# Expert rows in a two-layer network: stores on GpSimd's queue, gathers two pairs ahead in buffers of their own, the short stream first

## The chip, the cores and the metric

The kernel runs on one core of one Trainium2 chip. The metric is the device time of one execution in microseconds (us). In the profile PE is TensorE (PEld its weight loads), DVE is VectorE, ACT is ScalarE, POOL is GpSimd and SP is SyncE, which here only issues DMAs. A queue such as SPq or ACTq is the part of an engine that issues them.

## What is computed

The network has two blocks. The change touches the end of each of the two layers of the second block: a feed-forward part in which 16 experts each choose the tokens that they like best.

```
def _expert_choice_ffn(h, w_router, w_gate, w_up, w_down):
    b, t, d = h.shape
    cap = EC_CAPACITY_FACTOR * t // N_EXPERTS
    aff = jax.nn.softmax(jnp.einsum('btd,de->bte', h, w_router).astype(jnp.float32), axis=-1)
    vals, idx = lax.top_k(aff.transpose(0, 2, 1), cap)
    xg = jax.vmap(lambda hb, ib: hb[ib])(h, idx)
    hid = jax.nn.silu(jnp.einsum('becd,edf->becf', xg, w_gate)) * jnp.einsum('becd,edf->becf', xg, w_up)
    out = jnp.einsum('becf,efd->becd', hid, w_down) * vals[..., None].astype(h.dtype)
    return jax.vmap(lambda ob, ib: jnp.zeros((t, d), h.dtype).at[ib.reshape(-1)].add(ob.reshape(-1, d)))(out, idx)
```

The main stream x has 512 tokens of width 1024, so an expert takes 64 of them. The short stream cx (the context) has 256 tokens and an expert takes 32. Layer 0 runs the experts for both streams with the same weights; layer 1 needs only x. The result is scaled by a gate and added to the stream.

## The kernel before

All arithmetic of the experts is float32. Their weights are read from HBM once for each layer: for each pair of experts 8 pieces of 1 MB for gate and up, and 4 for down, 96 pieces in a layer. `ffn` sets the order: `gate_up` of pair 0, then for each further pair q its `gate_up` and `down` of pair q-1, and at last `down` of pair 7. The pieces go through SP's queue into a ring of slots: EW buffers of their own, and three more that lie in the memory of x and cx themselves, which are free once the streams have been written to HBM. A piece can only be issued when the matmuls on the piece that had its slot are done.

Before the experts, `route` works out the choices. ACT writes every token's row twice into an HBM tensor: scaled by its norm (`normed`, L1564) and as it is (`acc`, L1565; in layer 1 that is the output itself). DVE finds the best tokens by rounds of MAX8, FIND_INDEX8 and MATCH_REPLACE8, and makes the lists `gi` (rows to gather) and `si` (rows to add to).

For a pair, `gathered` (L1653) fetches the 128 rows of its two experts from `normed` by an indirect DMA on GpSimd's queue; PE transposes them (L1659) and ACT modulates them (L1662). In layer 0 one more gather on every second pair fetches the rows of cx for four experts. `gate_up` runs the matmuls of x (L1707) and of cx (L1716), `hidden` the activation, `down` those of x (L1730) and cx (L1742). DVE scales them (L1733, L1748) and `scatter` (L1762) adds them to `acc` by two indirect DMAs for each stream, also on GpSimd's queue; a scatter waits until the one before it into the same tensor has landed. After layer 0, `reload` reads the sums back (L1774), squares them on ACT (L1776) and transposes them on PE (L1780), the short stream first, and one `rsqrt` for all six row tiles follows. Then the mixers of layer 1 begin with matmuls at L472.

A scheduler at build time decides the order of instructions on each engine. It also gives each DMA one of eight completion counters: eight for the DMAs that SP and ACT issue together, and eight others for those of GpSimd. A DMA waits until the one that last had its counter has landed, whoever issued that one.

All row buffers (two in `route`, a gather's, a scatter's, two in `reload`) come from one pool of six, `row`.

Of the kernel before, what the change touches and what calls it, by code (L numbers as in the profile page):

```python
# [16 lines left out]
OP = mybir.AluOpType  # L17
# [204 lines left out]

EW = 12
FILL_NA = (0, 1) * 6
FILL_H = (1, (0, 1, 0, 1, 0, 1, 0), 1, 0)

# [6 lines left out]
class _K:  # L235
# [1287 lines left out]
    def route(self, l, v, x, nt, cap, state, got):  # L1523
# [30 lines left out]
        wk = self.tl("y", [16, 512])[:, :W]  # L1554
        yield
        for i in range(nt):
            raw, row = self.tl("row", [P, D]), self.tl("row", [P, D])
            for s in range(2):
                pq = self.pt("s")
                for k in range(4):  # L1560
                    ten.transpose(pq[:, k * P:(k + 1) * P], x[:, 4 * s + k, i * P:(i + 1) * P], self.idf)
                act.activation(row[:, s * 512:(s + 1) * 512], pq, AF.Copy, scale=rs[:, i:i + 1])
                act.activation(raw[:, s * 512:(s + 1) * 512], pq, AF.Copy)
            act.dma_start(self.normed[v][i * P:(i + 1) * P, :], row)  # L1564
            act.dma_start(self.acc[v][i * P:(i + 1) * P, :], raw)  # L1565

        val = self.s1(f"val{v}", [16, cap])
        idx = self.s1(f"idx{v}", [16, cap], U32)
# [77 lines left out]
        if need:  # L1646
            self.reload(x, cx)

    def gathered(self, l, v, gi, n):

        nc = self.nc
        row = self.tl("row", [P, D])
        nc.gpsimd.indirect_dma_start(row[:], None, self.normed[v][:, :], bass.IndirectOffsetOnAxis(ap=gi[:, n:n + 1], axis=0))  # L1653
        o = self.tl("xg", [P, KT, P])
        a2, b2 = self.mods[v]
        for s in range(2):
            pq = self.pt("t")
            for k in range(4):
                nc.tensor.transpose(pq[:, k * P:(k + 1) * P], row[:, (4 * s + k) * P:(4 * s + k + 1) * P], self.idf)  # L1659
            for k in range(4):  # L1660
                d = 4 * s + k
                nc.scalar.activation(o[:, d], pq[:, k * P:(k + 1) * P], AF.Identity, scale=a2[:, d:d + 1], bias=b2[:, d:d + 1])  # L1662
        return o

    def experts(self, l, acts, got, eload):
# [3 lines left out]
        ten, vec, act, pool = nc.tensor, nc.vector, nc.scalar, nc.gpsimd  # L1669
        self.mods = {v: self.mod_cols(l, v, 3, self.v(f"n2{l}")) for v in got}  # L1670
        two = 1 in got
        xg, hid = {}, {}

        def inputs(q):
            if q < 8:
                xg[0, q] = self.gathered(l, 0, got[0][0], q)
                if two and q % 2 == 0:
                    xg[1, q] = xg[1, q + 1] = self.gathered(l, 1, got[1][0], q // 2)

        def hidden(q, v, g, u, n):  # L1680

# [15 lines left out]
        def gate_up(q):  # L1697
            pg, pu = self.pt("g"), self.pt("g")
            pv = self.pt("o") if two else None
            x0 = xg[0, q]  # L1700
            for j in range(2):
                w = [[eload() for _ in range(2)] for _ in range(2)]
                for ps, wn in ((pg, w[0]), (pu, w[1])):
                    for k in range(4):
                        d = 4 * j + k
                        for e in range(2):
                            ten.matmul(ps[e * 64:(e + 1) * 64], x0[:, d, e * 64:(e + 1) * 64], wn[e][:, k],  # L1707
                                       start=d == 0, stop=d == 7)
                if two:
                    for k in range(4):  # L1710
                        d = 4 * j + k
                        for n in range(2):
                            for e in range(2):
                                r = (2 * n + e) * 32
                                c = (2 * (q % 2) + e) * 32
                                ten.matmul(pv[r:r + 32], xg[1, q][:, d, c:c + 32], w[n][e][:, k],  # L1716
                                           start=d == 0, stop=d == 7)
            hidden(q, 0, pg, pu, P)
            if two:
                hidden(q, 1, pv[:64], pv[64:], 64)  # L1720

        def down(q):
            w = [[eload() for _ in range(2)] for _ in range(2)]
            gi, si, val, gate = got[0]
            y = self.tl("row", [P, D])
            for j in range(2):
                ps = self.pt("s")
                for f in range(4):
                    for e in range(2):
                        ten.matmul(ps[e * 64:(e + 1) * 64], hid[0, q][:, f, e * 64:(e + 1) * 64], w[j][e][:, f],  # L1730
                                   start=f == 0, stop=f == 3)
                c = slice(j * 512, (j + 1) * 512)
                vec.scalar_tensor_tensor(y[:, c], ps, val[:, q:q + 1], gate[:, c], OP.mult, OP.mult)  # L1733
            self.scatter(0, y, si, q, 64)
            if two:
                gi, si, val, gate = got[1]
                ps = self.pt("a")
                for f in range(4):
                    for j in range(2):
                        for e in range(2):  # L1740
                            r = (2 * j + e) * 32
                            ten.matmul(ps[r:r + 32], hid[1, q][:, f, e * 32:(e + 1) * 32], w[j][e][:, f],  # L1742
                                       start=f == 0, stop=f == 3)
                y = self.tl("row", [P, D])
                for j in range(2):
                    r = slice(j * 64, j * 64 + 64)
                    c = slice(j * 512, (j + 1) * 512)
                    vec.scalar_tensor_tensor(y[:64, c], ps[r], val[r, q:q + 1], gate[r, c], OP.mult, OP.mult)  # L1748
                self.scatter(1, y, si, q, 32)

        inputs(0)
        for what, q in acts:
            if what == "gu":
                inputs(q + 1)
                gate_up(q)
            else:
                down(q)
# [8 lines left out]
    def reload(self, x, cx):  # L1766

        nc = self.nc
        ss = self.s1("ssr", [P, 6])
        ev = 0  # L1770
        for v, xs, nt, c0 in ((1, cx, 2, 0), (0, x, 4, 2)):
            for i in range(nt):
                row = self.tl("row", [P, D])
                nc.scalar.dma_start(row, self.acc[v][i * P:(i + 1) * P, :])  # L1774
                j = self.tl("row", [P, D])
                nc.scalar.activation(j, row, AF.Square, accum_out=ss[:, c0 + i:c0 + i + 1])  # L1776
                for s in range(2):
# [2 lines left out]
                        nc.tensor.transpose(pq[:, k * P:(k + 1) * P], row[:, (4 * s + k) * P:(4 * s + k + 1) * P], self.idf)  # L1780
                    d = xs[:, 4 * s:4 * s + 4, i * P:(i + 1) * P]
                    nc.vector.tensor_copy(d, pq.rearrange("p (k c) -> p k c", k=4))
        self.rsqrt(ss, 6, 1.0 / D, self.rs2)

    def block2(self, x, cx, rb, dram, out):
        self.rs2 = self.one("rs2", [P, 6])
        for l in range(DEPTH):
            need = l < DEPTH - 1
            with self.scope(v=3, z2=4, n=1, e3=5, sb=1, f3=9, h=16, t=5, tg=2, xc=1, wr=2, wh=2, wl=2, sm=2, s1=1):
                states = self.mixer2(l, x, cx, need, *rb)  # L1790
            self.normed = [dram.tile([n, D], F32, name=f"normed{l}{n}", tag=f"n{n}") for n in ((T, 256) if need else (T,))]
            self.acc = [dram.tile([n, D], F32, name=f"acc{l}{n}", tag=f"a{n}") for n in (T, 256)] if need else [out]
            with self.scope(ew=EW, row=6, xg=4, hid0=2, **({"hid1": 2} if need else {}), t=5, sm=2, s1=1):
                self.ffn(l, x, cx, need, states)
            rb = None, self.rs2

# [46 lines left out]
```

## Time and profile before

| what | us |
|---|---|
| median of 3 runs (3087.5 to 3098.31) | 3091.7 |
| the profiled execution | 3086.54 |
| its span, first to last instruction | 3084.8 |
| PE busy | 2844.5 (92%) |
| DVE busy | 1493.4 (48%) |
| ACT busy | 1164.3 (38%) |
| POOL busy | 256.3 (8%) |

The span is what the trace shows; 1.74 us of the execution lie around it. All times below are us from the start of the span. The experts of layer 0 run from about 2001 to 2339, the reload up to 2383, the mixers of layer 1 to 2795, its route and experts to the end. Busy PE is an average over stages with different limits, so each stage has to be read by itself.

### The profile page before, as it was taken

The page shows a single profiled execution, that of the slowest core. Times are in us where ns is not written, and L with a number is a line of the kernel's source. Part 1 is how long each engine was busy: PE and PEld are TensorE (multiplying, and loading weights), DVE is VectorE, ACT ScalarE, POOL GpSimd, SP SyncE. Part 2 cuts the span into 40 slices and gives each one's busy share as a digit, 9 for nine tenths or more (in the row PEclk, how much of TensorE's full clock was granted, in tenths as well). Part 3 has the DMA queues.
Part 4 walks back from the last instruction along what each step waited for, and adds up shares of the span by engine and source line. Part 5 has one row for each costly group of instructions (what it writes and reads, how often), then busy time and mean ns, then how long its engine had stood idle before and what let it go on. Part 6 is the DMA issues. An engine that isn't in the chain of part 4 may idle for free. (4 is left out here: it accounts for less than half of the span.)

```text
span 3084.8 us, 46595 instructions
## 1 busy us (share of the span) xinstructions
PE 2844.5 (92%) x18975; PEld 1935.1 (63%) x18976; DVE 1493.4 (48%) x3039; ACT 1164.3 (38%) x2410; POOL 256.3 (8%) x236
## 2 busy tenths in 40 slices
PE   8999999999999999999999999798896999996985
PEld 5676667876776667877766888523223767773321
DVE  4625686544535686636366466611113465574100
ACT  5523454433533454444454342421112463443210
POOL 0000031000000020100011010011111010000111
PEclk9999999999999999999999999799997999997999
DMA  4142424412233224421110111778884111118998
GB/s 146 48 167 73 143 97 171 151 60 71 69 123 115 97 97 163 164 83 50 48 33 28 56 43 36 287 282 328 322 325 112 54 42 52 51 51 339 410 406 308
DMA packets 97574, 439.54 MB, mean 142 GB/s; under 512 B 11216, under 2 KB 12496, under 8 KB 72784
## 3 DMA queue, kind: packets, MB, share of 16 engines
q1 hardware_dynamic: 86976, 401.09, 35.2%
q0 software_dynamic: 6640, 21.83, 3.1%
q10 hardware_dynamic: 3744, 13.63, 1.2%
q8 instruction: 150, 2.46, 0.3%
q14 instruction: 64, 0.52, 0.1%
HBM read 416.40 MB, written 20.97 MB: 142 GB/s over the span
## 5 line engine op out<-in xcount | busy, mean ns | idle before, releaser
L472 PE MATMUL psg<-h,wh 128*128 128x512 f32 x1616 | 653.1, 405 | 2.4 <-ACT z L1322 1.9
L473 PE MATMUL psg<-h,wh 128*128 128x512 f32 x1616 | 647.4, 401 | 0.0
L474 PE MATMUL psg<-h,wl 128*128 128x512 f32 x1616 | 646.9, 400 | 0.0
L462 DVE TENSOR_TENSOR wl<-wr,wh 128x1024 fp32r<-128x1024 f32 (+2 forms) x272 | 338.7, 1246 | 489.0 <-ACT wh L460 477.5
L460 ACT ACTIVATE wh<-wr 128x1024 fp32r<-128x1024 f32 (+2 forms) x272 | 281.0, 1034 | 606.9 <-PE psg L473 528.0
L472 PEld LDWEIGHTS psg<-h,wh 128*128 128x128 f32 x1616 | 305.1, 189 | 95.8 <-issue 24.6
L473 PEld LDWEIGHTS psg<-h,wh 128*128 128x128 f32 x1616 | 305.0, 189 | 74.5 <-issue 14.3
L474 PEld LDWEIGHTS psg<-h,wl 128*128 128x128 f32 x1616 | 305.3, 189 | 73.6 <-issue 12.4
L1707 PE MATMUL psg<-ew,xg 128*64 128x512 f32 x832 | 235.0, 629 | 16.9 <-DMA ew<-in_eu_dram 11.4
L472 PE MATMUL psg<-y,wh 128*128 128x256 f32 (+1 forms) x560 | 181.0, 324 | 2.7 <-ACT y L448 2.0
L473 PE MATMUL psg<-y,wh 128*128 128x256 f32 (+1 forms) x560 | 180.3, 322 | 0.0
L474 PE MATMUL psg<-y,wl 128*128 128x256 f32 (+1 forms) x560 | 178.5, 319 | 0.0
L1707 PEld LDWEIGHTS psg<-ew,xg 128*64 128x64 f32 x832 | 68.4, 144 | 150.2 <-issue 118.7
L1684 DVE SCALAR_TENSOR_TENSOR t<-t,psg 128x512 f32<-128x512 f32 x16 | 11.0, 688 | 306.2 <-ACT t L1683 306.2
L1662 ACT ACTIVATE xg<-pst,mB,mA 128x128 f32<-128x128 f32 x160 | 58.6, 466 | 164.9 <-PE pst L1659 164.8
L1007 ACT ACTIVATE t<-pst 128x512 f32<-128x512 f32 (+1 forms) x134 | 69.9, 557 | 125.4 <-PE pst L1004 122.5
L472 PEld LDWEIGHTS psg<-y,wh 128*128 128x128 f32 x560 | 107.0, 191 | 16.2 <-ACT y L448 2.4
L472 PE MATMUL psg<-f,wh 128*128 128x256 f32 (+1 forms) x360 | 113.3, 316 | 4.0 <-DVE x L557 1.8
L1730 PE MATMUL pss<-ew,hid 128*64 128x512 f32 x416 | 108.8, 598 | 5.3 <-DMA ew<-in_ed_dram 5.3
L473 PE MATMUL psg<-f,wh 128*128 128x256 f32 (+1 forms) x360 | 112.7, 313 | 0.8 <-DVE f L1242 0.8
L473 PEld LDWEIGHTS psg<-y,wh 128*128 128x128 f32 x560 | 107.3, 192 | 9.5 <-issue 2.1
L474 PE MATMUL psg<-f,wl 128*128 128x256 f32 (+1 forms) x360 | 111.5, 310 | 0.0
(462 smaller groups left out, 4489.8 us busy)
## 6 DMA issues: line engine op xcount, KB each, us to landing
ew<-in_eg_dram SPq DMA_DIRECT2D x52, 1024.0 KB, 12.0
ew<-in_eu_dram SPq DMA_DIRECT2D x52, 1024.0 KB, 11.7
ew<-in_ed_dram SPq DMA_DIRECT2D x52, 1024.0 KB, 11.3
wm<-in_wm_dram SPq DMA_DIRECT2D x96, 512.0 KB, 4.4
wr<-in_w_f_dram SPq DMA_DIRECT2D x92, 512.0 KB, 3.6
wr<-in_v_f_dram SPq DMA_DIRECT2D x60, 512.0 KB, 3.2
wr<-in_w_o_dram SPq DMA_DIRECT2D x32, 512.0 KB, 3.8
x<-in_eg_dram SPq DMA_DIRECT2D x10, 1024.0 KB, 14.4
```

The costliest lines, as they stand in the source:

```text
L460: nc.scalar.activation(hi, raw, AF.Copy)
L462: nc.vector.tensor_tensor(lo, raw, hi, OP.subtract)
L472: t.matmul(ps, a[0], b[0], start=first, stop=False)
L473: t.matmul(ps, a[0], b[1], start=False, stop=False)
L474: t.matmul(ps, a[1], b[0], start=False, stop=last)
L1007: self.nc.scalar.activation(pT[:, :w], pp[:, :w], AF.Copy)
L1662: nc.scalar.activation(o[:, d], pq[:, k * P:(k + 1) * P], AF.Identity, scale=a2[:, d:d + 1], bias=b2[:, d:d + 1])
L1684: vec.scalar_tensor_tensor(th, th, 1.0, g, OP.add, OP.mult)
L1707: ten.matmul(ps[e * 64:(e + 1) * 64], x0[:, d, e * 64:(e + 1) * 64], wn[e][:, k], start=d == 0, stop=d == 7)
L1730: ten.matmul(ps[e * 64:(e + 1) * 64], hid[0, q][:, f, e * 64:(e + 1) * 64], w[j][e][:, f], start=f == 0, stop=f == 3)
```

## The change

Six things change. (1) The stores of rows to `normed` and `acc` are issued by GpSimd instead of ACT. (2) Row buffers are two pools of four: `in` for raw rows, gathers and reloads, `row` for scaled rows and scatters. EW goes from 12 to 11, which makes room. (3) The gathers of pair q+2 are issued at the start of pair q, apart from their transposes. (4) In `gate_up` and `down` the short stream's matmuls stand ahead of the main stream's. (5) So its scatter does too. (6) `reload` has a `rsqrt` for each stream.

```
-EW = 12
+EW = 11
...
-            raw, row = self.tl("row", [P, D]), self.tl("row", [P, D])
+            raw, row = self.tl("in", [P, D]), self.tl("row", [P, D])
...
-            act.dma_start(self.normed[v][i * P:(i + 1) * P, :], row)
-            act.dma_start(self.acc[v][i * P:(i + 1) * P, :], raw)
+            nc.gpsimd.dma_start(self.normed[v][i * P:(i + 1) * P, :], row)
+            nc.gpsimd.dma_start(self.acc[v][i * P:(i + 1) * P, :], raw)
...
+    def gather(self, v, gi, n):
+
+        row = self.tl("in", [P, D])
+        self.nc.gpsimd.indirect_dma_start(row[:], None, self.normed[v][:, :],
+                                          bass.IndirectOffsetOnAxis(ap=gi[:, n:n + 1], axis=0))
+        return row
...
+        def fetch(q):
+            for v in range(1 + (two and q % 2 == 0)):
+                if q < 8:
+                    rows[v, q] = self.gather(v, got[v][0], q // 2 if v else q)
+
         def inputs(q):
...
+            for v in range(1 + (two and q % 2 == 0)):
+                if q < 8:
+                    xg[v, q] = xg[v, q + v] = self.modulated(v, rows.pop((v, q)))
...
+        fetch(0)
+        fetch(1)
         inputs(0)
         for what, q in acts:
             if what == "gu":
+                fetch(q + 2)
                 inputs(q + 1)
                 gate_up(q)
...
-                row = self.tl("row", [P, D])
+                row = self.tl("in", [P, D])
...
-        self.rsqrt(ss, 6, 1.0 / D, self.rs2)
+            c = slice(c0, c0 + nt)
+            self.rsqrt(ss[:, c], nt, 1.0 / D, self.rs2[:, c])
...
-            with self.scope(ew=EW, row=6, xg=4, hid0=2, **({"hid1": 2} if need else {}), t=5, sm=2, s1=1):
+            with self.scope(ew=EW, row=4, **{"in": 4}, xg=4, hid0=2, **({"hid1": 2} if need else {}), t=5, sm=2, s1=1):
```

Three places in the order of instructions matter below. The first is SP's queue at the beginning of layer 0's experts. `ew`, `x` and `cx` are the slots of weight pieces, `wr` a weight of the mixer ahead. DMAHW0 to 7 are the counters shared by SP and ACT, DMASW0 to 7 those of GpSimd; the number behind them has no meaning here. Before:

```order
L458 DMA wr_18119<-in_v_o_dram 128x768 [waits DMAHW1_49,DVE_49]
L1626 DMA ew_18234<-in_eg_dram 128x2048
L1626 DMA ew_18236<-in_eg_dram 128x2048 [waits DMAHW5_49,PE_49]
L1626 DMA ew_18238<-in_eu_dram 128x2048 [waits DMAHW6_49,DMASW1_49,Pool_49]
L1626 DMA ew_18240<-in_eu_dram 128x2048
L1626 DMA ew_18242<-in_eg_dram 128x2048 [waits DMAHW2_49]
L1626 DMA ew_18244<-in_eg_dram 128x2048 [waits DMAHW5_49,Pool_49]
L1626 DMA ew_18246<-in_eu_dram 128x2048 [waits DMAHW6_49]
L1626 DMA ew_18248<-in_eu_dram 128x2048 [waits DMAHW1_49]
L1626 DMA ew_18250<-in_eg_dram 128x2048 [waits DMAHW3_49]
L1626 DMA ew_18252<-in_eg_dram 128x2048 [waits DMAHW5_49]
```

And in the changed kernel:

```order
L458 DMA wr_17987<-in_v_o_dram 128x768 [waits DMAHW7_49,DVE_49]
L1626 DMA ew_18237<-in_eg_dram 128x2048
L1626 DMA ew_18239<-in_eg_dram 128x2048 [waits DMASW1_49,DVE_49,Pool_49]
L458 DMA wr_18049<-in_v_o_dram 128x768 [waits DMAHW0_49,DVE_49]
L1626 DMA ew_18241<-in_eu_dram 128x2048 [waits DMAHW5_49,PE_49]
L458 DMA wr_18119<-in_v_o_dram 128x768 [waits DMAHW6_49,DMAHW1_49,DVE_49]
L1626 DMA ew_18243<-in_eu_dram 128x2048
L1626 DMA ew_18245<-in_eg_dram 128x2048 [waits Pool_49]
L1626 DMA ew_18247<-in_eg_dram 128x2048
L1626 DMA ew_18249<-in_eu_dram 128x2048 [waits DMAHW2_49]
L1626 DMA ew_18251<-in_eu_dram 128x2048 [waits DMAHW3_49]
L1626 DMA ew_18253<-in_eg_dram 128x2048 [waits DMAHW4_49]
```

In the changed kernel the weight pieces take the counters one after the other (2, 3, 4), and the first three stand ahead of the last two loads of the mixer; before, they skip counters, which ACT's stores hold.

The second place is GpSimd's queue in the first pairs of layer 0. Names with 18206 and 18208 belong to the main stream, with 18207 and 18209 to the short one. Before:

```order
L1762 DMA acc_18208<-row_18866,si_3791_18510 512x1024
L1653 DMA row_18911<-normed_18206,gi_3790_18508 128x1024
L1762 DMA acc_18208<-row_18866,si_3791_18510 512x1024
L1762 DMA acc_18209<-row_18906,si_3796_18528 256x1024 x2
L1762 DMA acc_18208<-row_19044,si_3791_18510 512x1024
L1653 DMA row_19089<-normed_18206,gi_3790_18508 128x1024
L1762 DMA acc_18208<-row_19044,si_3791_18510 512x1024
L1762 DMA acc_18209<-row_19084,si_3796_18528 256x1024
L1653 DMA row_19110<-normed_18207,gi_3795_18526 128x1024
L1762 DMA acc_18209<-row_19084,si_3796_18528 256x1024
```

And in the changed kernel:

```order
L1564 DMA normed_18207<-row_18471 128x1024
L1565 DMA acc_18209<-in_18470 128x1024
L1652 DMA in_18567<-normed_18206,gi_3789_18509 128x1024
L1652 DMA in_18569<-normed_18207,gi_3794_18527 128x1024
L1652 DMA in_18571<-normed_18206,gi_3789_18509 128x1024
L1652 DMA in_18611<-normed_18206,gi_3789_18509 128x1024
L1652 DMA in_18613<-normed_18207,gi_3794_18527 128x1024
L1652 DMA in_18725<-normed_18206,gi_3789_18509 128x1024
L1652 DMA in_18916<-normed_18206,gi_3789_18509 128x1024
L1652 DMA in_18918<-normed_18207,gi_3794_18527 128x1024
L1652 DMA in_19096<-normed_18206,gi_3789_18509 128x1024
L1774 DMA acc_18209<-row_18888,si_3795_18529 256x1024 x2
```

The gathers (now L1652) up to pair 5 stand ahead of the first scatter (now L1774), and behind the last of twelve stores; before, the gather for the next pair stood behind a scatter of this one.

The third place is ACT's queue in `reload`. Before:

```order
L1774 DMA row_20057<-acc_18209 128x1024
L1776 ACTIVATE row_20059,ssr_20056<-row_20057 128x1024
L1774 DMA row_20073<-acc_18209 128x1024
L1776 ACTIVATE row_20075,ssr_20056<-row_20073 128x1024
L1774 DMA row_20089<-acc_18208 128x1024
L1776 ACTIVATE row_20091,ssr_20056<-row_20089 128x1024
```

And in the changed kernel:

```order
L1785 DMA in_20059<-acc_18209 128x1024
L1785 DMA in_20075<-acc_18209 128x1024
L1785 DMA in_20111<-acc_18208 128x1024
L1787 ACTIVATE row_20061,ssr_20058<-in_20059 128x1024
L1787 ACTIVATE row_20077,ssr_20058<-in_20075 128x1024
L1787 ACTIVATE row_20113,ssr_20058<-in_20111 128x1024
L1785 DMA in_20127<-acc_18208 128x1024
L1785 DMA in_20143<-acc_18208 128x1024
L1785 DMA in_20159<-acc_18208 128x1024
L1787 ACTIVATE row_20129,ssr_20058<-in_20127 128x1024
```

The loads go out three at a time; before, each waited behind the square of the row before it.

## Rows read from the trace of the kernel before

**Rows 1.** What PE waited for, 1955 to 2345: total us, times, longest.

```profile
PE pst L1659 <- DMA row<-normed,gi: 30.3, 8, 5.5
```

**Rows 2.** Chain that ended last, 2150 to 2345: start, us, what.

```profile
...
2212.46 10.61 DMA row<-normed,gi
...
2280.91 2.72 PE pss L1730 x10
...
2314.65 2.72 PE pss L1730 x10
...
```

**Rows 3.** PE in order of time, start of layer 0's experts.

```profile
...
2012.67 1.09 PE L1659 MATMUL pst<-const_sb,row 128*128 128x128 f32 x4 [5.49 <-DMA row<-normed,gi]
...
2020.33 3.65 PE L1707 MATMUL psg<-ew,xg 128*64 128x512 f32 x14
...
2041.77 1.20 PE L1659 MATMUL pst<-const_sb,row 128*128 128x128 f32 x8
...
2064.41 2.79 PE L1730 MATMUL pss<-ew,hid 128*64 128x512 f32 x10
...
```

**Rows 4.** What SP's queue waited for, whole span.

```profile
...
SPq L1626 <- DMA acc<-row: 44.5, 4, 26.2
...
SPq L1626 <- DMA out_dram<-row: 25.9, 3, 19.9
...
```

**Rows 5.** SP's queue in order of time.

```profile
...
1912.45 23.04 SPq L458 DMA_DIRECT2D wr<-in_v_o_dram  x5
...
1945.67 26.90 SPq L1626 DMA_DIRECT2D ew<-in_eu_dram  x2
...
2840.49 0.33 SPq L1626 DMA_DIRECT2D ew<-in_eu_dram  x1
...
```

**Rows 6.** Stretches: length, busy PE, PEld, DVE, ACT, POOL, clock, DMA share, GB/s.

```profile
1945.00:1970.00 25.00, 21.93 (x152) 16.74 (x150) 17.35 (x58) 10.33 (x21) 0.00 (x0) 1.00 0.44 181
1970.00:2001.00 31.00, 12.96 (x78) 9.31 (x78) 23.13 (x73) 12.85 (x24) 1.03 (x1) 0.55 1.00 382
...
2028.00:2281.00 253.00, 230.18 (x1278) 75.75 (x1276) 32.80 (x46) 43.33 (x105) 34.46 (x27) 0.95 0.88 329
...
2841.00:3058.00 217.00, 184.72 (x802) 61.97 (x798) 20.76 (x29) 26.99 (x64) 21.13 (x16) 0.98 1.01 406
```

**Rows 7.** POOL in order of time.

```profile
1991.21 1.03 POOL L1653 DMA_INDIRECT row<-normed,gi  x1 [100.92 <-DVE y L1575]
2008.27 0.97 POOL L1653 DMA_INDIRECT row<-normed,gi  x1 [16.03 <-DMA cx<-in_eu_dram]
...
2341.64 1.41 POOL L1762 DMA_INDIRECT acc<-row,si  x1 [3.55 <-DMA acc<-row,si]
...
2344.24 1.10 POOL L1137 DMA_DIRECT2D f<-in_namask_dram  x1
...
2824.14 1.03 POOL L1653 DMA_INDIRECT row<-normed,gi  x1 [81.64 <-DMA normed<-row]
```

**Rows 8.** PE in order of time, end of layer 0's experts and reload.

```profile
...
2335.55 3.62 PE L1742 MATMUL psa<-ew,hid 128*32 128x512 f32 x26
...
2383.19 0.80 PE L472 MATMUL psg<-y,wh 128*128 128x256 f32 x2 [2.03 <-ACT y L448]
...
```

**Rows 9.** ACT and its queue in order of time, around layer 0's experts.

```profile
...
1946.09 0.85 ACT L460 ACTIVATE wh<-wr 128x768 fp32r<-128x768 f32 x1
...
1968.26 0.34 ACTq L1564 DMA_DIRECT2D normed<-row  x1
...
2353.23 0.33 ACTq L1774 DMA_DIRECT2D row<-acc  x1
...
2374.51 1.06 ACT L1776 ACTIVATE row<-row 128x1024 f32<-128x1024 f32 x1 [3.06 <-DMA row<-acc]
...
```

**Rows 10.** DVE in order of time, last list of layer 0's route, list of layer 1's.

```profile
...
1996.05 0.16 DVE L1592 CAST gi<-pst 128x4 uint32<-128x4 f32 x1 [0.75 <-PE pst L1588]
...
2820.62 0.17 DVE L1592 CAST gi<-pst 128x8 uint32<-128x8 f32 x1 [0.94 <-PE pst L1588]
...
```

More of the change, by code (lines that the diff above doesn't have):

```diff
@@ L1647, in ffn, with modulated @@
             self.reload(x, cx)
-    def gathered(self, l, v, gi, n):
+    def gather(self, v, gi, n):
[3 more added lines that the diff above has]
+        return row
+    def modulated(self, v, row):
         nc = self.nc
-        row = self.tl("row", [P, D])
-        nc.gpsimd.indirect_dma_start(row[:], None, self.normed[v][:, :], bass.IndirectOffsetOnAxis(ap=gi[:, n:n + 1], axis=0))
         o = self.tl("xg", [P, KT, P])
@@ L1671, in experts @@
         two = 1 in got
-        xg, hid = {}, {}
+        rows, xg, hid = {}, {}, {}
+        def fetch(q):
+            for v in range(1 + (two and q % 2 == 0)):
+                if q < 8:
+                    rows[v, q] = self.gather(v, got[v][0], q // 2 if v else q)
         def inputs(q):
[L1675 to L1678, printed above, removed]
+            for v in range(1 + (two and q % 2 == 0)):
+                if q < 8:
+                    xg[v, q] = xg[v, q + v] = self.modulated(v, rows.pop((v, q)))
         def hidden(q, v, g, u, n):
@@ L1702, in gate_up @@
                 w = [[eload() for _ in range(2)] for _ in range(2)]
[L1703 to L1708, printed above, removed]
                 if two:
@@ L1717, in gate_up @@
                                            start=d == 0, stop=d == 7)
+                    if j:
+                        hidden(q, 1, pv[:64], pv[64:], 64)
+                for ps, wn in ((pg, w[0]), (pu, w[1])):
+                    for k in range(4):
+                        d = 4 * j + k
+                        for e in range(2):
+                            ten.matmul(ps[e * 64:(e + 1) * 64], x0[:, d, e * 64:(e + 1) * 64], wn[e][:, k],
+                                       start=d == 0, stop=d == 7)
             hidden(q, 0, pg, pu, P)
-            if two:
-                hidden(q, 1, pv[:64], pv[64:], 64)
         def down(q):
             w = [[eload() for _ in range(2)] for _ in range(2)]
[L1724 to L1734, printed above, removed]
             if two:
@@ L1749, in down @@
                 self.scatter(1, y, si, q, 32)
+            gi, si, val, gate = got[0]
+            y = self.tl("row", [P, D])
+            for j in range(2):
+                ps = self.pt("s")
+                for f in range(4):
+                    for e in range(2):
+                        ten.matmul(ps[e * 64:(e + 1) * 64], hid[0, q][:, f, e * 64:(e + 1) * 64], w[j][e][:, f],
+                                   start=f == 0, stop=f == 3)
+                c = slice(j * 512, (j + 1) * 512)
+                vec.scalar_tensor_tensor(y[:, c], ps, val[:, q:q + 1], gate[:, c], OP.mult, OP.mult)
+            self.scatter(0, y, si, q, 64)
+        fetch(0)
+        fetch(1)
         inputs(0)
@@ L1769, in reload @@
         ss = self.s1("ssr", [P, 6])
-        ev = 0
         for v, xs, nt, c0 in ((1, cx, 2, 0), (0, x, 4, 2)):
             for i in range(nt):
-                row = self.tl("row", [P, D])
+                row = self.tl("in", [P, D])
                 nc.scalar.dma_start(row, self.acc[v][i * P:(i + 1) * P, :])
```

## Prediction

> **What bounds the kernel now.** I read the waits of PE first, since PE is busy for 92% of the span and what it waits for is where time can come from. Around layer 0's experts it waits mainly for one thing, the gathered rows: 30.3 us in eight pieces, none over 5.5 [rows 1]. The chain of waits says why a gather is late. It stands on GpSimd's queue behind a scatter, and under the weight traffic it takes up to 10.61 us to land; the next transposes wait for it [rows 2]. The same chain has what a pair costs without a gather: between the `down` of pairs 5 and 6 lies only the `gate_up` of pair 7, for which nothing more is gathered, and that is 2314.65 - 2280.91 = 33.74 us [rows 2]. PE in order of time gives a pair with gathers: the first `down` begins at 2064.41 [rows 3], five pairs before 2280.91, so (2280.91 - 2064.41) / 5 = 43.3 us.
>
> Next I read SP's waits, because SP carries all weights. It waited 44.5 us in layer 0 and 25.9 us in layer 1 for stores that ACT had issued [rows 4]. No weight piece reads what these stores write; what the two share is a completion counter, as the order of SP's queue shows. In time: two pieces took 26.90 us to issue from 1945.67 [rows 5], and in that stretch the DMA engines were busy for only 0.44. Right behind it the share is 1.00, because all that was held back and the stores now come together, and TensorE's granted clock is 0.55, about its lower level (1.2 GHz), with PE busy for 12.96 of 31 us [rows 6].
>
> Last come the windows of the two expert stages. In layer 0's pairs the DMA share is 0.88 at 329 GB/s. In layer 1's it is 1.01 at 406 GB/s with PE busy 184.72 of 217 us [rows 6]. So layer 0 waits for gathers with room left on the DMA engines, and layer 1 is bound by the weight stream: gathers issued earlier buy nothing inside it.
>
> **The change part by part.**
>
> *Gathers two pairs ahead (layer 0).* They leave GpSimd some 70 us (two pairs) before their transposes, against the 10.61 us that one takes [rows 2]. PE keeps the transposes: 8 take 1.20 us [rows 3], and a pair has 8 for x and in every second pair 8 for cx, so 1.8 us on average. A pair then takes 33.74 + 1.8 = 35.5 us, and five pairs save 5 x (43.3 - 35.5) = 39 us. This is more than the rows of waits hold, because the clock and the order of work behind each wait are slower too (0.95 in the window [rows 6]). The bound on the other side is the DMA engines: 253 us at 0.88 are 222.6 us of transfers in 253 / 43.3 = 5.84 pairs, or 38.1 us per pair. If that binds, five pairs save 26 us. I take 39, since the stream is ahead of PE by the ring: 14 pieces are more than the 12 of a pair, and being 38.1 - 35.5 = 2.6 us late per pair uses up 13 us of that lead in five pairs. Term: -39 (-26 to -39).
>
> *Stores on GpSimd's queue (layer 0's start).* Twelve stores leave ACT. The trace has a plain DMA of 1.10 us on GpSimd, [rows 7], and about 0.3 us passes between two, so 12 take 17 us. The first rows are ready at 1968.26 [rows 9], the last list at 1996.05 [rows 10]: 27.8 us, in which GpSimd does nothing else, so the stores cost nothing there. What they free is SP: weight pieces no longer share a counter with them, go out during the idle stretch (0.44) and are through before the rows of cx are stored. Before, the gather of cx left at 2008.27, 12.2 us after its list, because the stores that it reads had to land in a crowd; 4.4 us later PE had it [rows 3, 7]. With quiet engines it leaves with its list, at about 1996. The transposes and the first matmuls follow at the same distance, so the stage starts 12 us earlier. Bounds: if the three pieces that go into the slots of x and cx crowd the gather, it takes the 10.61 us of rows 2 in place of 4.4, and 6 remain; if the list is a little earlier as well, 14. Term: -12 (-6 to -14).
>
> *Short stream first, and reload.* Before, the last expert matmul ended at 2335.55 + 3.62 = 2339.17; call it T. The first load of `reload` went out at 2353.23 (T + 14.1), the last square ran at 2374.51 and the mixers began at 2383.19 (T + 44.0) [rows 8, 9]. Six row tiles thus took (2374.51 - 2353.23) / 6 = 3.5 us each, one behind another, and 8.7 us of closing work followed. Afterwards cx's scatters are out of the way before T. Those of x are two, and the second waits 3.55 us for the first to land and takes 1.41 [rows 7]; with the scaling on DVE and the second landing the loads of x can leave at about T + 11.5. The tiles of cx are done by then. Of x three loads go at once, so four tiles take two rounds of 3.5 us and three squares of 1.06 [rows 9], or 10.2. T + 11.5 + 10.2 + 8.7 = T + 30.4: a gain of 13.6. Bounds: if only the two tiles of cx drop out, 7; if the squares hide too, 17. Term: -13.6 (-7 to -17).
>
> *Layer 1.* Its gather left at 2824.14, held by a store that it reads [rows 7], 3.5 us after its list [rows 10]; the first slot of a weight piece came free at 2840.49 [rows 5]. From there the weight stream sets the end. Without the crowd the gather leaves with its list, 3.5 us earlier, and I take another 3.5 for landing, about halfway to the 6.2 between 10.61 and 4.4 us. Against that stands the slot less: one more piece of 1.05 MB has to come after the first slot is free, 2.6 us at 406 GB/s. Term: -7 + 2.6 = -4.4 (-7 to +3).
>
> *What costs nothing.* Three weight pieces now stand on SP ahead of the last two loads of the mixer's weight. They take 3 x 2.6 = 7.7 us of DMA time. The last of those loads was issued by 1912.45 + 23.04 = 1935.49 [rows 5], and ACT touched it at 1946.09 [rows 9], so 10.6 us cover it. Without that cover it would cost up to 5 us (bound). ACT loses 20 issues of about 0.34 us [rows 9], off its critical work.
>
> Sum: -39 - 12 - 13.6 - 4.4 = -69.0. The profiled execution took 3086.5, 5.2 below the median shown, so 3017.5 for it and 3091.7 - 69.0 = 3022.7 for the median: 3023.
>
> **A rule against the change.** While DVE worked on its lists (23.13 of 31 us busy [rows 6]), GpSimd's gather at 1991.21 issued in 1.03 us, and the one at 2008.27, with DVE idle, in 0.97 [rows 7]. The Trainium skill, page "SBUF — State Buffer", section "Who interferes with whom", says the opposite may happen: DVE in its two-port modes locks GpSimd out, so that DMAs which GpSimd issues stall, and they belong on another queue. By that rule the stores would be held up; by the row they are not. One gather is little evidence, so it is a rival below.
>
> **Rivals.**
>
> 1. *The DMA engines bind layer 0's pairs* (38.1 us each). For it: 0.88 busy already. Against: the ring's lead. Then -69 + 13 = -56: 3036. Chance 0.17.
> 2. *The change doesn't free the start*: the weight queue is held by something else than the stores' counters. For it: 0.44 might be the mixer's end, in which slots are not free. Against: SP's waits name the stores. The start gains nothing and layer 1 only loses its slot: -39 - 13.6 + 2.6 = -50: 3042. Chance 0.14.
> 3. *Stores are held until DVE's lists are done.* Twelve then go out from 1996.05, 1.4 us each, and the gather at 2012.9 instead of 2008.27 (+4.6); layer 1's eight from 2820.62 to 2831.8 instead of 2824.14 (+7.7, +2.6 for the slot): -39 + 4.6 - 13.6 + 10.3 = -38: 3054. It is the mechanism of the rule cited above. Against it is the 1.03 us. Chance 0.06.
> 4. *Slower: stores that each hold GpSimd's queue.* If a store waits on the queue until its write is through, the gathers, which stand behind twelve and eight of them, come late. With p us for one, 20 x (p + 0.3) - 27.8 has to eat the 69 and another 9: p = 5.0, or 6.4 if layer 1 covers as many us as layer 0. Against it: the row has 1.10 [rows 7]. For it: SP's queue was held 26.90 us by two pieces [rows 5], so a queue can stand behind a DMA. At p = 6.5 the kernel takes 3023 + 108 = 3131. Chance 0.03.
>
> **How the numbers follow.** Main case 0.57, rivals 0.17, 0.14, 0.06 and 0.03, and 0.03 for a larger gain than any term allows. The main case's own range: all terms at their best give -39 - 14 - 17 - 7 = -77 or 3015, the two largest at their worst (-26, -6) 3042; with a run-to-run spread of 3 that is 3012 to 3045. The whole range has to take in rivals 1 to 3, and below it the larger gain and the spread of single runs (4 to 7 us around the median): 3004 to 3056. What the runs cannot tell from no change is about 0.3%, 9 us; all cases but the fourth lie 38 us or more below. Faster 0.95, within that 0.02, slower 0.03.
>
> **What would show it.** Right: PE no longer waits for gathered rows; SP no longer waits for stores of `acc` or the output; `down` begins every 35.5 us; T lies near 2288, the mixers start 30 us after it and layer 1's first slot comes free about 70 us earlier than before. A period of 38 us with a DMA share near 1.00 shows rival 1; a gather of cx after 2005 shows 2 or 3, with stores waiting on GpSimd for 3. The prediction fails above all if the DMA engines, once PE asks for more, deliver no more than 329 GB/s: then a pair stays near 43 us and only 30 us come from the ends.

## The result, and the profile after

| | before | after |
|---|---|---|
| median, us (4 runs each) | 3091.8 | 3040.1 (3037.17 to 3043.31) |
| profiled execution, us | 3086.54 | 3043.31 |
| its span, us | 3084.8 | 3041.3 |

The ratio is 0.9831 (0.9811 to 0.9851): 51.7 us faster. That lies in the range, but 17 us short of the 69 in the sum. The two profiled executions lie 43.2 apart, since one was below its median and the other above.

The waits of PE, 1955 to 2345, in the changed kernel. Against [rows 1] the line for gathered rows is gone:

```profile
PE pst L1791 <- DMA in<-acc: 13.3, 2, 12.1
PE pss L1561 <- ACT in L1563: 7.4, 6, 3.2
PE pst L1587 <- DVE fi L1580: 7.0, 2, 3.6
PE pst L1553 <- DVE aff L1550: 2.3, 2, 2.0
```

The windows (columns as in [rows 6]). The changed kernel reaches the route of layer 0 5.8 us later (see below), so the first two are the first two of [rows 6] moved by 5.78 us; the third is not moved and holds the stores:

```profile
1950.78:1975.78 25.00, 22.37 (x153) 17.26 (x152) 17.25 (x57) 10.53 (x21) 1.12 (x2) 0.98 0.57 237
1975.78:2006.78 31.00, 16.05 (x99) 10.62 (x100) 21.49 (x74) 15.49 (x32) 10.12 (x15) 0.69 0.94 354
1970.00:2001.00 31.00, 14.22 (x95) 10.29 (x94) 25.65 (x99) 14.56 (x28) 7.43 (x13) 0.69 0.82 320
2028.00:2230.00 202.00, 202.00 (x1162) 64.56 (x1162) 29.38 (x41) 41.00 (x99) 32.25 (x25) 1.00 0.97 367
2800.00:3015.00 215.00, 177.54 (x782) 59.80 (x780) 21.53 (x30) 26.57 (x64) 19.31 (x15) 0.98 1.02 409
```

The DMA share in the first stretch rose from 0.44 to 0.57 and the crowd behind it fell from 1.00 to 0.94. SP has issued all its eleven pieces by 1946.64, where before two of them took until 1972.57 [rows 5]:

```profile
1944.52 1.65 SPq L1626 DMA_DIRECT2D ew<-in_eg_dram  x2
1946.20 0.44 SPq L1626 DMA_DIRECT2D ew<-in_eu_dram  x1
```

In the pairs PE is busy all the time, at the full clock, with the DMA engines at 0.97. They deliver 367 GB/s and not 329, so they had room.

GpSimd in order of time, changed kernel: first and last store, the gathers of x and cx, the gather for pair 5, the first scatter.

```profile
1974.32 0.59 POOL L1564 DMA_DIRECT2D normed<-row  x1 [76.77 <-ACT row L1562]
...
1989.38 0.53 POOL L1565 DMA_DIRECT2D acc<-in  x1
1995.29 1.02 POOL L1652 DMA_INDIRECT in<-normed,gi  x1 [5.37 <-DVE gi L1592]
2001.15 0.97 POOL L1652 DMA_INDIRECT in<-normed,gi  x1 [4.84 <-DMA normed<-row]
...
2038.38 0.95 POOL L1652 DMA_INDIRECT in<-normed,gi  x1 [2.22 <-PE pst L1664]
2065.07 1.36 POOL L1774 DMA_INDIRECT acc<-row,si  x1 [25.74 <-DVE row L1746]
```

Stores take 0.53 to 0.59 us each, and a gather now waits for the transposes that empty its buffer ("PE pst"), not for a scatter.

To compare kernels whose starts differ, I cut each span at the same events. R is the first DVE instruction of the route in layer 0. Of before and after:

```profile
1963.29 0.16 DVE L309 TENSOR_SCALAR rq_a<-pst 128x4 f32<-128x4 f32 x1 [0.73 <-PE pst L402]
```

```profile
1969.07 0.16 DVE L309 TENSOR_SCALAR rq_a<-pst 128x4 f32<-128x4 f32 x1 [0.73 <-PE pst L402]
```

Up to the mixer's last weight loads the order on SP's queue is the same in both, so the 5.8 us between them are drift of the run. D0 and D5 are the first matmuls of `down` for pairs 0 and 5, T the end of the last expert matmul, M the first L472 of layer 1's mixers, R1 the route of layer 1. D5 before, on PE in order of time:

```profile
2280.84 2.79 PE L1730 MATMUL pss<-ew,hid 128*64 128x512 f32 x10
```

And in the changed kernel D0, D5, the last matmul before T, and M:

```profile
2058.02 1.04 PE L1740 MATMUL psa<-ew,hid 128*32 128x512 f32 x2
...
2241.24 1.04 PE L1740 MATMUL psa<-ew,hid 128*32 128x512 f32 x2
...
2303.89 1.02 PE L1754 MATMUL pss<-x,hid 128*64 128x512 f32 x2
...
2336.87 0.80 PE L472 MATMUL psg<-y,wh 128*128 128x256 f32 x2 [0.77 <-ACT y L448]
```

and R1 on DVE, before and after:

```profile
2796.47 0.16 DVE L309 TENSOR_SCALAR rq_a<-pst 128x4 f32<-128x4 f32 x1 [1.72 <-PE pst L402]
```

```profile
2757.06 0.16 DVE L309 TENSOR_SCALAR rq_a<-pst 128x4 f32<-128x4 f32 x1 [1.72 <-PE pst L402]
```

This table is the main reading of the study. It holds the profiled execution of every kernel; the medians are from the timed runs, and the last column is the median of the kernel before, timed beside it.

| kernel | R-D0 | D0-D5 | D5-T | T-M | M-R1 | R1-end | median | before |
|---|---|---|---|---|---|---|---|---|
| before | 101.1 | 216.4 | 58.3 | 44.0 | 413.3 | 288.3 | 3091.8 | |
| after | 89.0 | 183.2 | 63.7 | 32.0 | 420.2 | 284.2 | 3040.1 | 3091.8 |
| stores_only | 90.1 | 216.3 | 62.5 | 44.9 | 415.7 | 286.5 | 3085.3 | 3092.9 |
| stores_back | 96.5 | 183.2 | 63.7 | 32.9 | 418.0 | 282.6 | 3045.9 | 3092.9 |
| x_first | 87.7 | 178.5 | 62.5 | 33.5 | 415.5 | 284.8 | 3032.0 | 3092.9 |
| gathers_only | 92.6 | 178.5 | 62.5 | 36.5 | 417.0 | 283.5 | 3032.6 | 3092.9 |
| pools_only | 93.6 | 178.5 | 62.5 | 35.5 | 414.6 | 283.9 | 3032.7 | 3089.6 |
| down_first | 88.0 | 178.3 | 64.5 | 32.6 | 418.0 | 284.6 | 3031.9 | 3089.6 |
| ahead_one | 90.2 | 183.2 | 63.7 | 32.4 | 418.4 | 284.6 | 3038.9 | 3089.6 |
| ew12 | 92.6 | 183.2 | 69.9 | 33.5 | 421.9 | 287.8 | 3056.1 | 3089.6 |
| ew11_only | 92.6 | 217.9 | 62.5 | 45.0 | 421.8 | 284.3 | 3087.5 | 3092.4 |
| shared8 | 94.2 | 216.4 | 62.5 | 45.2 | 417.8 | 284.1 | 3082.5 | 3092.4 |
| in2 | 93.9 | 178.5 | 62.5 | 40.1 | 416.9 | 288.9 | 3047.5 | 3092.4 |
| pools_stores | 86.2 | 178.5 | 62.6 | 35.5 | 415.8 | 284.8 | 3032.6 | 3092.4 |

### The profile page after: what moved, and what is told of

Same layout as the page of the kernel before. It is cut to its first block, busy times and chain, and to the rows that moved or that the text cites. A ratio compares the mean times of both kernels' runs of the same rounds, so it can differ in the third digit from the quotient of the medians.

```text
span 3041.3 us, 46563 instructions
## 1 busy us (share of the span) xinstructions
PE 2846.7 (94%) x18975; PEld 1936.7 (64%) x18976; DVE 1493.5 (49%) x3051; ACT 1164.2 (38%) x2410; POOL 267.0 (9%) x256
## 5 line engine op out<-in xcount | busy, mean ns | idle before, releaser
L472 PE MATMUL psg<-h,wh 128*128 128x512 f32 x1616 | 654.1, 405 | 0.7 <-DVE x L1078 0.4
L472 PEld LDWEIGHTS psg<-h,wh 128*128 128x128 f32 x1616 | 305.2, 189 | 94.8 <-issue 24.6
L1727 PE MATMUL psg<-ew,xg 128*64 128x512 f32 x832 | 222.7, 609 | 23.8 <-DMA ew<-in_eu_dram 13.1
L472 PE MATMUL psg<-y,wh 128*128 128x256 f32 (+1 forms) x560 | 181.1, 324 | 1.5 <-ACT y L448 0.8
L472 PE MATMUL psg<-f,wh 128*128 128x256 f32 (+1 forms) x360 | 115.1, 321 | 4.1 <-DVE x L557 1.8
L472 PEld LDWEIGHTS psg<-y,wh 128*128 128x128 f32 x560 | 107.9, 193 | 14.8 <-DVE x L1078 2.1
L474 PEld LDWEIGHTS psg<-y,wl 128*128 128x128 f32 x560 | 107.9, 193 | 6.1 <-issue 0.6
L1004 PE MATMUL pst<-const_sb,t 128*128 128x128 f32 x488 | 84.5, 284 | 4.5 <-DVE t L1232 3.3
```

The costliest lines, as they stand in the source:

```text
L472: t.matmul(ps, a[0], b[0], start=first, stop=False)
L474: t.matmul(ps, a[1], b[0], start=False, stop=last)
L1004: ten.transpose(pp[:, (2 * i + a) * P:(2 * i + a + 1) * P], ps[a][:, c:c + P], self.idf)
```

## The experiments

The theory at the start was the prediction's: gathers ahead of scatters speed up the pairs, stores off ACT speed up the start and layer 1, the short stream's order speeds up the exit. The first four kernels take these apart.

**stores_only.** Before, with the stores on GpSimd:

```diff
-            act.dma_start(self.normed[v][i * P:(i + 1) * P, :], row)
-            act.dma_start(self.acc[v][i * P:(i + 1) * P, :], raw)
+            nc.gpsimd.dma_start(self.normed[v][i * P:(i + 1) * P, :], row)
+            nc.gpsimd.dma_start(self.acc[v][i * P:(i + 1) * P, :], raw)
```

> The kernel before with only the stores of rows moved to GpSimd's queue. Theory (the stores' completion counters held the weight queue): SP's waits for acc<-row (44.5 us) and out_dram<-row (25.9 us) are gone, layer 0's experts start about 12 us earlier and layer 1's first slot comes free about 7 us earlier, pairs stay at 43.3 us: about 19 us off 3091.8, so 3073. Rival (the weight queue was held by something else, and the early start of the changed kernel comes from the gathers' new place in GpSimd's order): 3089 to 3094.

3085.3, ratio 0.9972 (0.9963 to 0.9981): 12 us above what was expected. SP's waits for the stores are gone and R-D0 falls by 11.0, as the theory has it; but layer 1 gains 1.8 in place of 7, and D5-T costs 4.2 that nobody had counted.

**stores_back.** After, with those two lines as before.

> The changed kernel with only the stores back on ACT's queue. Theory (the stores' counters): SP waits for stores again, layer 0's experts start about 12 us later, layer 1's first slot comes free about 7 us later, the pairs keep their 36.6 us: 3040.1 + 17 to 19 = 3057 to 3059. Rival (the stores are not the cause): 3040 within 4.

3045.9, ratio 0.9845 (0.9832 to 0.9858) to before: neither side. R-D0 is 7.6 longer than after, layer 1 is not longer at all. So the stores are worth less beside the other parts than alone.

**x_first.** After, with the loops of `gate_up` and `down` in the order of before:

```diff
             for j in range(2):
                 w = [[eload() for _ in range(2)] for _ in range(2)]
+                for ps, wn in ((pg, w[0]), (pu, w[1])):
...
                 if two:
...
-                    if j:
-                        hidden(q, 1, pv[:64], pv[64:], 64)
-                for ps, wn in ((pg, w[0]), (pu, w[1])):
```

> The changed kernel with the main stream's matmuls and scatters ahead of the short stream's again; stores, gathers and the two rsqrt stay. Theory (the short stream's activation now interrupts the main stream's matmuls, which costs PE about 1 us in a pair and some 4 us at the end): a pair takes about 35.6 us instead of 36.64, the last matmul comes 8 to 10 us earlier relative to the first down, and the mixers of layer 1 begin about 10 us later after it than the 31.9 us of the changed kernel: 3040.1 within 4. Rival (the pair's extra time is the transposes' own and the order costs nothing): the period stays 36.6, only the gain after the last matmul is lost, 3050.

3032.0, ratio 0.9810 (0.9795 to 0.9824). The pairs are 4.7 us faster, as expected, but the exit is only 1.5 longer, not 10. So both the theory and its rival were wrong about the exit: the order buys next to nothing there. It costs more than it brings.

**gathers_only.** x_first with the stores on ACT and one `rsqrt`, which is before with the two pools, the slot less and the gathers ahead.

> The kernel before with only the gathers issued two pairs ahead into buffers of their own (and the slot less that makes room); stores on ACT, main stream first, one rsqrt. Theory (late gathers made the pairs slow): PE no longer waits for gathered rows in the pairs, a pair takes 35.6 to 36.7 us instead of 43.3, the start and the exit stay as before, layer 1 loses 2.6 us with its slot: -33 to -38 + 2.6, so 3056 to 3061. Rival (the DMA engines bind the pairs): 38.1 us a pair or more with a DMA share near 1.00, 3068 or more.

3032.6, ratio 0.9810 (0.9794 to 0.9826): some 25 us better than expected, and as good as all six parts but the order. D0-D5 came out as expected (178.5, 35.7 a pair), but the start gained 8.5, the exit 7.5 and layer 1 4.8, for which the prediction had named the stores and the short stream. What is left in it is three things, the pools, the slot less and the place in the order, and the next kernel drops the last.

**pools_only.** Before with two pools and a slot less; gathers and order as they were:

```diff
-EW = 12
+EW = 11
...
-            raw, row = self.tl("row", [P, D]), self.tl("row", [P, D])
+            raw, row = self.tl("in", [P, D]), self.tl("row", [P, D])
...
-        row = self.tl("row", [P, D])
+        row = self.tl("in", [P, D])
...
-            with self.scope(ew=EW, row=6, xg=4, ...):
+            with self.scope(ew=EW, row=4, **{"in": 4}, xg=4, ...):
```

> The kernel before with only the two pools of four row buffers and the slot less; the gathers keep their place in the order, the stores stay on ACT. Theory A (a gather was late because of its place behind a scatter on GpSimd's queue): the pairs stay at 42 to 43 us and PE waits for gathered rows as before; reload still gains some 7 us since three loads can go at once, layer 1 loses 2.6: 3092.9 - 5 = about 3088. Theory B (a gather was late because it shared six buffers with the scatters and had to wait for one): the pairs fall to about 36 us, the start moves 8 us as in the kernel with gathers ahead alone: about 3035 to 3045.

3032.7, ratio 0.9821 (0.9806 to 0.9837). The time is that of theory B. GpSimd in order of time shows that the gathers now leave early, though the code asks for them where it did before:

```profile
2001.32 0.97 POOL L1653 DMA_INDIRECT in<-normed,gi  x1 [9.35 <-ACT xg L1662]
...
2035.48 0.95 POOL L1653 DMA_INDIRECT in<-normed,gi  x1 [21.62 <-PE pst L1659]
2039.53 0.95 POOL L1653 DMA_INDIRECT in<-normed,gi  x1 [3.10 <-PE pst L1659]
2066.21 1.48 POOL L1762 DMA_INDIRECT acc<-row,si  x1 [25.73 <-DVE row L1733]
```

Nine gathers stand ahead of the first scatter, as in the changed kernel, against five before. With a pool of their own, the scheduler puts them there by itself. So A was right that the place behind a scatter made a gather late, and wrong that only the code moves it.

**down_first.** After, with the main stream first in `gate_up` alone.

> The changed kernel with the main stream first in gate_up again, the short stream first in down alone. Theory (the 0.95 us that a pair takes longer in the changed kernel than with the main stream first is the short stream's activation cutting into the main stream's gate and up matmuls): the pairs take 35.7 us as with the main stream first, and the mixers begin 32 us after the last expert matmul as in the changed kernel: 3040.1 - 5 to 3040.1 - 9, that is 3031 to 3035. Rival (the order in down costs it): pairs stay at 36.6 us, 3038 to 3042.

3031.9, ratio 0.9817 (0.9800 to 0.9834). The pairs are back at 34.7 and 37.1 us in turn, where the changed kernel has 35.7 and 38.0. So the extra 0.95 us comes with the order in `gate_up`. There the short stream's transposes cut into the main stream's matmuls; PE in order of time, changed kernel:

```profile
2074.76 7.09 PE L1727 MATMUL psg<-ew,xg 128*64 128x512 f32 x32
...
2085.34 0.64 PE L1727 MATMUL psg<-ew,xg 128*64 128x512 f32 x1
2085.35 0.64 PE L1727 MATMUL psg<-x,xg 128*64 128x512 f32 x1
...
2087.97 1.02 PE L1727 MATMUL psg<-ew,xg 128*64 128x512 f32 x2
2088.92 0.46 PE L1701 MATMUL pst<-const_sb,t 64*128 64x64 f32 x4
2089.31 1.08 PE L1727 MATMUL psg<-x,xg 128*64 128x512 f32 x4
...
2092.79 1.02 PE L1727 MATMUL psg<-cx,xg 128*64 128x512 f32 x2
2093.75 1.04 PE L1740 MATMUL psa<-ew,hid 128*32 128x512 f32 x2
2094.72 0.66 PE L1701 MATMUL pst<-const_sb,t 128*128 128x128 f32 x4
2095.31 3.63 PE L1740 MATMUL psa<-ew,hid 128*32 128x512 f32 x30
```

In the run of 32 that isn't cut (from 2074.76, the next line starts at 2081.77) a matmul takes 7.01 / 32 = 0.22 us. The cut run starts its matmuls in twos, 0.01 us apart. Two of them stand alone ahead of the cut and hold PE for 0.95 us (2087.97 to 2088.92), two more at its end for 0.96 (2092.79 to 2093.75). The run takes 8.41 us, of which 0.39 are the transposes, so a cut costs 1.0. Right behind it the main stream's transposes cut the short matmuls of `down` (2094.72), and the two ahead of that cut take 0.97. In down_first only the matmuls of `down` are cut:

```profile
2054.89 2.76 PE L1740 MATMUL psa<-ew,hid 128*32 128x512 f32 x18
2057.58 0.46 PE L1701 MATMUL pst<-const_sb,t 64*128 64x64 f32 x4
2057.97 1.92 PE L1740 MATMUL psa<-ew,hid 128*32 128x512 f32 x14
```

x_first has one cut in a pair as well (in `down`, 2053.82). The changed kernel has two, and the second is the 0.95 us.

**ahead_one.** After, with `fetch(q + 1)` at the start of pair q and no `fetch(1)` ahead.

> The changed kernel with gathers issued one pair ahead in place of two (fetch(q + 1) at the start of pair q). Theory (only the landing of some 10 us has to be covered, and the gather's place in GpSimd's order does not reach behind the scatter of the pair before): no wait for gathered rows in the pairs, 36.6 us each, 3040 within 4. Rival (one pair ahead puts the gather behind scatters again and it lands late): PE waits 4 us or more in each pair, 3055 to 3065.

3038.9, ratio 0.9836 (0.9820 to 0.9852), and the same D0-D5. With pools of their own, how far ahead the code asks is of no account.

**ew12.** After, with EW = 12, `row=3` and `in=3`.

> The changed kernel with a slot more (EW 12) and a row buffer less in each pool (3 and 3). Theory (layer 1 is bound by the weight stream, so a slot more saves the loading of one piece, 2.6 us, after the first slot is free; layer 0 is bound by PE and does not care): layer 1 from its list to the end is 2 to 3 us shorter, 3037 to 3038. Rival (three buffers are too few, so gathers and scatters wait for one another): PE waits for gathered rows again, 3043 or more.

3056.1, ratio 0.9887 (0.9869 to 0.9906): 16 slower than after, which neither side expected in this place. PE doesn't wait for gathers in the pairs. The losses are at the start (3.6), in the last pairs (6.2) and in layer 1 (3.6), where the slot was to help. GpSimd there:

```profile
2785.95 0.53 POOL L1564 DMA_DIRECT2D normed<-row  x1 [8.51 <-ACT row L1562]
...
2795.04 1.04 POOL L1652 DMA_INDIRECT in<-normed,gi  x1 [8.04 <-DMA normed<-row]
```

Its list is ready at 2790.88. The gather waits 4.2 us for a store to land; with 11 slots it leaves 0.95 us after its list (2781.22 and 2782.17). The last store of `normed` left late itself: GpSimd stood 8.51 us for its row, against 1.32 in the changed kernel, which may come from the three row buffers. Which of the three edits made the last pairs slower stays open.

The last four ask whether it is the slot, the number of buffers or who owns them.

**ew11_only.** Before with `EW = 11` alone.

> The kernel before with EW 11 alone; one pool of six row buffers. Theory (the buffers of their own made the gathers early, the slot less only thins the weight pieces in front of the stores): the pairs stay at 43 us with PE waiting for gathered rows, the start may move up to 8 us (in the kernel with separate pools it moved 7.5 without the stores), layer 1 changes by -3 to +3: 3081 to 3092. Rival (fewer weight pieces in flight made the gathers land in time): pairs of 36 us, 3040 to 3050.

3087.5, ratio 0.9984 (0.9975 to 0.9994). The pairs stay slow, but R-D0 falls by 8.5 and R1-end by 4.0: a slot less gives here what the prediction gave to the stores, and SP's wait for the stores of `acc` is gone too, with these still on ACT. That for the stores of the output falls from 25.9 us to 13.7.

**shared8.** Before with `EW = 11` and `row=8`.

> The kernel before with EW 11 and one shared pool of eight row buffers, the same memory as the two pools of four. Theory (what matters is that a gather does not take over a buffer that a scatter has used; a shared pool hands them round in program order, and GpSimd's order with eight is the order of the kernel before): pairs of 42 to 43 us, as with EW 11 alone within 5 us. Rival (more buffers are enough): pairs of 36 us, 3032 to 3045.

3082.5, ratio 0.9973 (0.9961 to 0.9985). D0-D5 is that of before to a tenth, with the same memory as two pools of four. GpSimd, and the waits of PE:

```profile
2066.76 1.48 POOL L1762 DMA_INDIRECT acc<-row,si  x1 [60.35 <-DVE row L1733]
2068.54 1.00 POOL L1653 DMA_INDIRECT row<-normed,gi  x1 [0.30 <-issue]
```

```profile
PE pst L1659 <- DMA row<-normed,gi: 26.6, 7, 4.8
```

The gather for pair 3 leaves 0.30 us behind the first scatter and the trace names no buffer that it waits for.

**in2.** pools_only with `in=2`.

> The kernel with the two pools, but only two buffers for raw rows and gathers (EW 11, stores on ACT, order of before). Theory (ownership counts, not number): seven gathers stand ahead of the first scatter instead of nine, and a gather still leaves as soon as PE has transposed the one two before it: pairs of 35.7 to 37 us; reload loads two rows at once instead of three, some 3 us: 3032.7 + 1 to + 6. Rival (four are needed to be early): PE waits for gathered rows 3 us or more in a pair, 3050 or more.

3047.5, ratio 0.9858 (0.9842 to 0.9874). Two buffers do for the pairs (178.5), so ownership counts there: ew11_only has the same six buffers and the same slots in one pool, and takes 217.9. Number counts elsewhere, more than expected: T-M is 4.6 longer than in pools_only with two loads at a time in place of three, and R1-end 5.0 longer. The loads in `reload`, pools_only and in2:

```profile
2310.73 1.57 ACTq L1774 DMA_DIRECT2D in<-acc  x3
```

```profile
2310.74 1.08 ACTq L1774 DMA_DIRECT2D in<-acc  x2
```

**pools_stores.** pools_only with the stores on GpSimd.

> The kernel with the two pools and the stores on GpSimd's queue; gathers where they stood in the code, main stream first, one rsqrt. Theory (issuing the gathers two pairs ahead in the code does nothing, since with buffers of their own the scheduler puts them ahead by itself): same GpSimd order of gathers and the same pairs of 35.7 us as with the main stream first and the gathers ahead in the code, the start 5 us earlier than with the stores on ACT: 3028 to 3033. Rival (the code's order matters): PE waits for gathered rows, 3036 or more.

3032.6, ratio 0.9811 (0.9797 to 0.9825), with the pairs of x_first. It has the shortest start of all (86.2), which does not show against pools_only in the medians.

## Why the prediction came out as it did

The range held, and the steps partly held for other reasons than those given. Of the signs named ahead, PE's waits for rows and SP's for stores went. A `down` came every 36.6 us, not 35.5, T stood at 2304.91, not 2288, and the mixers followed 32.0 us after it.

**Pairs: right in size, half right in what held the gather.** The 35.5 us a pair were measured as 35.7 with the main stream first: -38 against -39. That a late gather "stands on GpSimd's queue behind a scatter" held (shared8, 2068.54). The step that failed is the cure: issuing it two pairs ahead did nothing beside pools of its own (pools_only, ahead_one), and what moved it was the pool. With 11 slots and the same number of buffers, five pairs take 217.9 us in one pool and 178.5 in two (six buffers, ew11_only and in2), or 216.4 and 178.5 (eight, shared8 and pools_only). Why a shared pool holds the gather back is argued and not shown: the code asks for the row of pair 0's scatter ahead of the one for pair 3's gather, and a pool handed out in that order would give the order seen on GpSimd. By this reading gathers issued two pairs ahead in the code could have been early in a shared pool too; no kernel tried that.

The bound by the DMA engines (rival 1) was not reached. In x_first PE is busy throughout the pairs, though the DMA share is 1.00:

```profile
2050.00:2220.00 170.00, 170.00 (x1008) 55.37 (x1002) 27.31 (x38) 33.24 (x80) 29.02 (x22) 1.00 1.00 377
```

So the 38.1 us, a share of 0.88 taken for a fixed amount of transfers, were no bound for these five pairs. Whether the ring's lead shrank meanwhile was not read.

**Short stream first: the failed size.** The prediction gave it a gain and no cost. In `gate_up` it takes 0.95 us a pair, 4.7 over the five, and D5-T is 1.2 longer than with the main stream first. So the pairs came to -33.2 in the changed kernel, against the -39 of the sum. The exit's -12.0 against -13.6 was nearly right as a sum, but 8.5 of it are the four buffers of `in` (pools_only), through the three loads at a time; the rest is two `rsqrt`, gathers, stores and order, 1.5 of it the order. For the whole the order is a loss: 4.7 + 1.2 - 1.5 = 4.4 us by the stages, 8 by the medians of x_first and down_first, whose intervals overlap that of the changed kernel, so that only the loss in the stages is clear.

**Start: -12.2 against -12.** Right, and the stores on ACT did hold it up (stores_only: -11.0, with SP's waits gone). Counted from R, the gather of cx left 12.9 us earlier than before (2001.15 here, 2008.27 before), though not with its list, which was ready at 1998.80, but 2.35 us after it. The row of that gather in [rows 7] names a weight piece for the memory of cx as the end of its wait, not a store; which of them it waited for is not shown. The slot less alone also gives -8.5, and it clears SP's wait for `acc` as well; the two do not add. Rival 2 did not happen. Nor did rival 3: while DVE was busy for 25.65 of 31 us, the stores took 0.53 to 0.59 us on GpSimd. What the Trainium skill says in "SBUF — State Buffer", "Who interferes with whom", of DMAs from GpSimd that stall under DVE in its two-port modes is not seen here; the trace does not show in which mode DVE ran. With 0.59 for the price p of a store, rival 4 was far off.

**Layer 1: -4.1 against -4.4, by luck, of the wrong parts.** The slot less was put at +2.6; alone it gives -4.0. The stores were put at -7; alone they give -1.8, and beside the pools +0.9 to +1.6. A microsecond or two between single profiles may be chance, but all kernels with 11 slots have 282.6 to 284.8 here except in2 (288.9), and the three with 12 slots 286.5 to 288.3. That the slot less helps by thinning what stands in front of the stores fits ew12's gather, but the two kernels differ in buffers too.

**Not in the sum:** D5-T. It is 62.5 to 64.5 us in every other kernel than ew12 (69.9) and 58.3 in before. In the rows of D5-T the main and the short stream's matmuls change places more often than before, also in stores_only, where their order in the code is that of before:

```profile
2326.09 1.04 PE L1742 MATMUL psa<-ew,hid 128*32 128x512 f32 x2
2327.06 1.07 PE L1730 MATMUL pss<-ew,hid 128*64 128x512 f32 x2
2328.06 1.05 PE L1742 MATMUL psa<-ew,hid 128*32 128x512 f32 x4
```

Each short piece holds PE for some 1.0 us, as in the rows of 2087.97; why the scheduler mixes them there was not tested. Then M-R1, where no instruction was meant to change: 413.3 before, 414.6 to 421.9 in the others. Its granted clock was 0.98 before and 0.96 after:

```profile
2336.87:2757.00 420.13, 400.81 (x3472) 309.92 (x3473) 250.63 (x534) 194.80 (x378) 32.56 (x34) 0.96 0.21 71
```

against, before,

```profile
2383.19:2796.47 413.28, 392.52 (x3473) 304.80 (x3474) 248.27 (x532) 195.13 (x378) 32.43 (x34) 0.98 0.19 66
```

I found no cause in the change for it. All other kernels lie above before there, by 1.3 us (pools_only) to 8.6 (ew12), each in a single profile, so the cause stays open.

The weight pieces ahead of the mixer's last loads cost nothing that can be seen: R moved by 5.8 us, but the same DVE instructions already stood 3.2 us later at 41 us and 7.3 at 1570 (1569.68 before, 1576.95 after). In all: 5.8 - 12.2 - 33.2 + 5.4 - 12.0 + 6.9 - 4.1 = -43.4, to a tenth the difference of the two spans (43.5).

No kernel beats the others clearly: pools_only, the smallest edit, and x_first, down_first, gathers_only and pools_stores all lie at 3032 to 3033, some 7 us below the changed kernel, with intervals that overlap its own.

## What to carry to other kernels

When a transfer is late, ask first which others share its pool of buffers: here a pool shared by early loads and late stores tied them together, and two more buffers did not loosen that. Give loads a pool of their own and look at what the scheduler then does before moving issues by hand. And a reorder that gains at the end of a stage can be paid for in every round of it.

## What was unexpected of the hardware

More prefetch was slower: with a weight slot less (ew11_only), the start of layer 0's experts took 8.5 us less and the end of layer 1 4.0 us, although layer 1 moves its weights at 406 to 409 GB/s with a DMA share above 1.00. The whole kernel gained only 4.9 us by the medians. Whether fewer pieces in front of the stores did that or other counters was not separated. And a plain store on GpSimd took 0.53 us, half of the 1.10 in [rows 7].
